# A transformer block on one core: later parts of the modulation loaded at longer intervals and summed later, splits of q, k, v first in line, both tiles' first norm ahead

## Chip, cores and metric

The kernel runs on one core of one Trainium2 chip. The metric is device time of one execution in microseconds (us), as the median of several runs. The profile is one execution, recorded by the hardware profiler; its times are microseconds from the start of its span.

## What is computed

One block over 256 tokens of width 1024, in float32. A vector `c` is turned into six rows of 1024 numbers, which shift, scale and gate the two halves of the block:

```python
mod = silu(c) @ w_ada + b_ada
sh_m, sc_m, gt_m, sh_f, sc_f, gt_f = split(mod, 6)
h = rms_norm(x, g_mix) * (1 + sc_m) + sh_m
qa, ka, va, qb, kb, vb, gate_logits = split(h @ w_in)    # six times 512, and 2048
oa = moba_attention(qa, ka, va, rel_bias)     # 8 heads, one block of 256: causal softmax with a bias
ob = stick_breaking_attention(qb, kb, vb)     # 8 heads
g_a, g_b = split(sigmoid(gate_logits))
mixed = (g_a * (oa @ w_br_moba) + g_b * (ob @ w_br_sb)) @ w_out
x = x + gt_m * mixed
h2 = rms_norm(x, g_ffn) * (1 + sc_f) + sh_f
u_val, u_gate = split(causal_conv3(h2 @ w_up))           # 2 times 2816
x = x + gt_f * ((gelu(u_gate) * u_val) @ w_down)
return rms_norm(x, g_final)
```

## The kernel before

**Precision.** Each float32 matrix is split into a high part (a cast to fp32r on ACT: `wh_`, `hh`, `qk` and so on) and a low part (the rest, subtracted on DVE: `wl_`, `hl`). A product is three matmuls on PE: high by high, high by low, low by high (`mm3`, L166). `split` (L144, L145) does it for weights, `hilo` (L150, L151; with a scale L153, L154) for what PE leaves in PSUM.

**Phase A**, up to about 63 us, is ordered by hand (`manual_schedule`, L63). `square` (L326) and `turn` scale each of the two token tiles by its norm and transpose it into `xT`. Then, for each of eight blocks of 128 columns, `row_sums` and `column_sums` make the first norm's shift and scale from `w_ada`, `modulated` (L444) makes `hh`, and `products` multiplies by rows of `w_in` (loaded as `raw_wA`) into the PSUM banks `pA` (q and k of the moba heads) and `pV` (v).

**From there on** a scheduler orders the instructions of each engine, by priorities that follow the order in which the code issues them. An engine takes its instructions strictly in that order. A `Stream` of units feeds PE: gate0, gate1, qkb0 and qkb2 (q and k of the stick-breaking heads, pairs 0 and 1, then 2 and 3), vb, gate2, gate3, ya, yb, out, up, down. A unit is two blocks of 128 rows of weights; `Stream.ahead` splits weights two units ahead. Weights come through three buffers `raw`. One unit on one token tile (or on one half, for qkb) is one event, and after each event `tick` lets every task under way take a step. Tasks are generators; `yield n` puts the next step n events later. PSUM has pools of 3 banks (`mm`, the stream's results), 1 (`pp`) and 4 (`sm`, all else).

**The tasks that the change touches.** `moba_pair` (L598 and on) has four instances, pair 0 to 3: scores in PSUM, then on DVE the bias and the maximum (`mx`, L607 to L609), on ACT the exponential (`sb`, L612) and the normalisation (L616), transposes on PE, and a split into `ph` and `pl`. `QK.place` (L549) takes `ps_qkb`, the result of qkb0 or qkb2, out of its bank and splits it into the tile `qk`. The first half (q) and the second (k) have a bank each, so with three banks the second half of qkb2 needs the bank that the first half of qkb0 held. `v_operand` (L560) does the same for v.

`modulation` (L731) makes the later rows: gt_m (named gtm; by `bcast_part`, which spreads the sums over the partitions with two matmuls `bc_gtm` on PE, L723), shf and scf for the second norm (each ends in eight short matmuls on PE, `ps_shf` and `ps_scf`, L739), and after the out stage gtf. Each row is summed from eight loads of 512 KB of `w_ada`, issued by SP through a pool of two buffers (`adap`), in `ada_part`:

```python
for k in range(KT):
    while stream.events < starts[k]:
        yield 1
    w.append(adap.tile([P, D], F32, tag="ada", name=f"ada_{nm}{k}"))
    pin(nc.sync.dma_start(w[k], w_ada[k * P:(k + 1) * P, base:base + D]))
    if k:
        mac(k - 1)
yield 3
mac(KT - 1)
```

`mac` is one DVE instruction over 128x1024 (`acc_gtm`, `acc_shf`, `acc_scf`; L696 for the first, L698 for the other seven). In the out stage `out_put` adds the residual, and makes the second norm, which uses `ps_shf` and `ps_scf` through the tile `ab2`.

## Time and profile before

| | us |
|---|---|
| median of 3 runs | 431.73 (431.01 to 436.56) |
| the profiled execution, device time | 431.41 |
| its span, first to last instruction | 429.7 |
| PE busy | 407.5 |
| DVE busy | 318.5 |
| ACT busy | 255.6 |

The device time of the profiled execution is 1.7 us over its span, and 0.3 us under the median. In a timeline row the numbers are start and duration; what stands in brackets is the idle time of that engine just before and what ended it. Durations of matmuls are modelled and overlap; the distance between two starts is what one costs. PEclk is TensorE's granted clock, 1.00 being 2.4 GHz and 0.50 being 1.2 GHz.

### The profile page before, as it was taken

Reading aid. Unit: us, or ns where it says so; the run is one execution under the profiler, and the core shown is the slowest. Engines: PE = TensorE matmul, PEld = TensorE weight load, DVE = VectorE, ACT = ScalarE, POOL = GpSimd, SP = SyncE. Lnnn points to the kernel's source line nnn. Section 1 sums busy time; section 2 is a strip of 40 time slices with the busy share of each in tenths; the row PEclk is TensorE's granted clock in tenths of the full one; section 3 lists DMA queues with packets and bytes.
Section 4 is the critical chain, followed back from the end, with each engine's and each line's share of the span. In section 5 each row is a group of like instructions: output and inputs, shape, how many; then the busy total and the mean of one; then the engine's idle time right before and its main releaser. Section 6 shows DMA issues by size and latency. Waiting matters only on the chain.

```text
span 429.7 us, 6803 instructions
## 1 busy us (share of the span) xinstructions
PE 407.5 (95%) x2636; PEld 357.5 (83%) x2636; DVE 318.5 (74%) x476; ACT 255.6 (59%) x407; POOL 25.1 (6%) x62
## 2 busy tenths in 40 slices
PE   7898999999699899999997999999999999999993
PEld 6786887899598787888875899999999999888882
DVE  2745578896779877997668779999898888546333
ACT  4425577875777779934355758666676666433312
POOL 2700000000001000000041000000000000000001
PEclk9999999999699999999998999999999999999997
DMA  8999988996368384775646685777376555573102
GB/s 275 333 319 333 356 306 290 327 309 223 125 237 300 112 286 146 274 238 224 194 123 221 188 299 201 233 255 261 135 217 202 174 194 195 151 276 116 45 2 98
DMA packets 67912, 94.45 MB, mean 220 GB/s; under 512 B 2573, under 2 KB 46736, under 8 KB 67879
## 3 DMA queue, kind: packets, MB, share of 16 engines
q1 hardware_dynamic: 66967, 91.82, 65.3%
q10 hardware_dynamic: 576, 1.57, 1.0%
q0 software_dynamic: 336, 0.62, 0.4%
q8 instruction: 21, 0.34, 0.3%
q14 instruction: 12, 0.10, 0.1%
HBM read 92.94 MB, written 1.06 MB: 219 GB/s over the span
## 4 chain that ended last, share of the span: by engine, by line
PE 60%; DMA 13%; DVE 12%; ACT 9%; issue 4%; POOL 1%; SPq 0%; POOLq 0%; DVEq 0%; ACTq 0%
PE ps_up L258 21%; PE ps_down L170 14%; DMA ada_gtm<-in_w_ada_dram 5%; PE pA L407 5%; PE ps_out L170 4%; DMA ada_shf<-in_w_ada_dram 4%; PE ps_up L170 3%; PE ps_ya L170 3%; PE ps_yb L170 3%; PE pV L412 2%; DMA raw_wA<-in_w_in_dram 2%; PE cs L392 2%; DMA ada_gtf<-in_w_ada_dram 2%; PE warm L121 2%; DVE wl_gate L145 1%
## 5 line engine op out<-in xcount | busy, mean ns | idle before, releaser
L144 ACT CAST wh_up<-raw_up 128x1024 fp32r<-128x1024 f32 x44 | 46.1, 1049 | 26.3 <-PE ps_up L258 20.5
L258 PE MATMUL ps_up<-h2h__2317,wh_up 128*128 128x256 f32 x320 | 57.7, 282 | 0.0
L258 PE MATMUL ps_up<-h2l__2318,wh_up 128*128 128x256 f32 x320 | 57.4, 281 | 0.0
L258 PE MATMUL ps_up<-h2h__2317,wl_up 128*128 128x256 f32 x320 | 57.4, 281 | 0.0
L145 DVE TENSOR_TENSOR wl_up<-raw_up,wh_up 128x1024 fp32r<-128x1024 f32 x42 | 51.0, 1218 | 7.7 <-ACT wh_up L144 7.5
L258 PEld LDWEIGHTS ps_up<-h2h__2317,wh_up 128*128 128x128 f32 x320 | 46.4, 188 | 0.2
L258 PEld LDWEIGHTS ps_up<-h2l__2318,wh_up 128*128 128x128 f32 x320 | 46.3, 188 | 0.0
L258 PEld LDWEIGHTS ps_up<-h2h__2317,wl_up 128*128 128x128 f32 x320 | 46.3, 188 | 0.0
L145 DVE TENSOR_TENSOR wl_down<-raw_down,wh_down 128x1024 fp32r<-128x1024 f32 x22 | 26.9, 1224 | 25.5 <-ACT wh_down L144 25.5
L144 ACT CAST wh_down<-raw_down 128x1024 fp32r<-128x1024 f32 x22 | 23.1, 1050 | 32.2 <-PE ps_down L170 23.7
L939 DVE SCALAR_TENSOR_TENSOR cv<-ps_up,wc,cv 128x255 f32<-128x255 f32 (+1 forms) x80 | 34.3, 475 | 1.3 <-ACT cv L933 0.8
L170 PE MATMUL ps_down<-wh_down,hl_a 128*128 128x512 f32 x88 | 34.8, 395 | 0.0
L170 PE MATMUL ps_down<-wl_down,hh_a 128*128 128x512 f32 x88 | 34.8, 395 | 0.0
L170 PE MATMUL ps_down<-wh_down,hh_a 128*128 128x512 f32 x88 | 34.8, 395 | 0.0
L170 PE MATMUL ps_gate<-wh_gate,hh 128*128 128x512 f32 x64 | 26.1, 407 | 1.2 <-DVE vbl L151 1.2
L170 PE MATMUL ps_gate<-wl_gate,hh 128*128 128x512 f32 x64 | 25.2, 394 | 0.0
L170 PE MATMUL ps_gate<-wh_gate,hl 128*128 128x512 f32 x64 | 25.2, 396 | 0.0
L933 ACT ACTIVATE cv<-ps_up,vc,wc 128x256 f32<-128x256 f32 x40 | 20.4, 564 | 5.2 <-PE ps_up L258 5.2
L145 DVE TENSOR_TENSOR wl_gate<-raw_gate,wh_gate 128x1024 fp32r<-128x1024 f32 x16 | 19.4, 1226 | 1.6 <-ACT wh_gate L144 1.6
L487 ACT CAST whA<-raw_wA 128x1024 fp32r<-128x1024 f32 (+1 forms) x9 | 8.5, 949 | 19.9 <-DMA raw_wA<-in_w_in_dram 19.9
L170 PEld LDWEIGHTS ps_down<-wh_down,hl_a 128*128 128x128 f32 x88 | 16.5, 188 | 4.0
L170 PEld LDWEIGHTS ps_down<-wh_down,hh_a 128*128 128x128 f32 x88 | 16.6, 188 | 3.9
(270 smaller groups left out, 899.4 us busy)
## 6 DMA issues: line engine op xcount, KB each, us to landing
raw_up<-in_w_up_dram SPq DMA_DIRECT2D x44, 512.0 KB, 5.1
raw_down<-in_w_down_dram SPq DMA_DIRECT2D x10, 1024.0 KB, 5.1
ada<-in_w_ada_dram SPq DMA_DIRECT2D x16, 512.0 KB, 7.4
raw_gate<-in_w_in_dram SPq DMA_DIRECT2D x8, 1024.0 KB, 5.1
raw_wA<-in_w_in_dram SPq DMA_DIRECT2D x8, 768.0 KB, 9.2
raw_qkb<-in_w_in_dram SPq DMA_DIRECT2D x8, 512.0 KB, 6.6
ada_gtm<-in_w_ada_dram SPq DMA_DIRECT2D x8, 512.0 KB, 4.7
ada_shf<-in_w_ada_dram SPq DMA_DIRECT2D x8, 512.0 KB, 6.5
```

The source lines that it names most:

```text
L121: nc.tensor.matmul(warm[:, 0:P], ones, ident, start=True, stop=True)
L144: nc.scalar.copy(wh[:, :n], t[:, a:a + n])
L145: (lo or nc.vector).tensor_sub(wl[:, :n], t[:, a:a + n], wh[:, :n].bitcast(F32))
L170: nc.tensor.matmul(ps, sx(k)[:, sl], w[:, c0:c0 + n], start=first and i == 0, stop=last and i == 2)
L258: nc.tensor.matmul(st.ps[f // 2][:, f % 2 * S:(f % 2 + 1) * S], wi[:, kk * 512 + f * P:kk * 512 + (f + 1) * P], sx(k0 + kk), start=first a ...
L392: nc.tensor.matmul(cs[g, 0:S].rearrange("p (i f) -> p i f", i=2), cw[:, k, :], ads[j][:, :, k, :], start=k < 4, stop=k >= 4)
L407: nc.tensor.matmul(psqk[f // 2][:, f % 2 * S:(f % 2 + 1) * S], wp[0][n == 2][:, f * P:(f + 1) * P], (hh, hl, hh)[n][:, j, :], start=j == 0 ...
L412: nc.tensor.matmul(psv[t], (hh, hl, hh)[n][:, j, t * P:(t + 1) * P], wp[1][n == 2][:, 0:512], start=j == 0 and n == 0, stop=j == KT - 1 an ...
L487: nc.scalar.copy(wh[i][:, a:a + n], wws[j][:, i * 1024 + a:i * 1024 + a + n])
L933: nc.scalar.activation(ct[:, b, :], tp[:, b * S:(b + 1) * S], AF.Identity, bias=bconv[:, fb:fb + 1], scale=wc[:, 88 + fb:89 + fb])
L939: nc.vector.scalar_tensor_tensor(ct[:, b, d:], tp[:, b * S:(b + 1) * S - d], wc[:, (2 - d) * 44 + fb:(2 - d) * 44 + fb + 1], ct[:, b, d:], ...
```

## The change

Four edits. `turn` no longer copies: both token tiles are scaled and transposed first, into the banks of `mm` (before: of `sm`), and the copies to `xT` come later (`put_xT`); a `warm_up(4)` between them is gone, and the banks `pA` and `pV` are taken after that. In `ada_part` the sum of load k-1 comes two events behind the issue of load k (before: at once), and the last one four events behind (before: three). The splits in `QK.place` and `v_operand` get a higher priority. The loads start at events 2 + int(3.2 i) (before: 3 + int(2.5 i)), i counting the 24 loads of gtm, shf and scf.

```diff
-    def turn(t, ss, copy):
+    def turn(t, ss):
         r = rstd_of(ss, f"n1_{t}")
         for half in range(2):
             sl = slice(half * 512, (half + 1) * 512)
             nc.vector.tensor_scalar(xs[t][:, sl], xs[t][:, sl], r, None, op0=ALU.mult)
+        tps = [bank(mm, f"xt{t}{half}") for half in range(2)]
+        for j in range(KT):
+            nc.tensor.transpose(tps[j // 4][:, j % 4 * P:(j % 4 + 1) * P], xs[t][:, j * P:(j + 1) * P], ident)
+        return tps
+
+    def put_xT(t, tps, copy):
         for half in range(2):
-            tp = bank(sm, f"xt{t}{half}")
-            for a in range(4):
-                j = 4 * half + a
-                nc.tensor.transpose(tp[:, a * P:(a + 1) * P], xs[t][:, j * P:(j + 1) * P], ident)
-            copy(xT[:, 4 * half:4 * half + 4, t * P:(t + 1) * P], tp.rearrange("p (a b) -> p a b", a=4))
+            copy(xT[:, 4 * half:4 * half + 4, t * P:(t + 1) * P], tps[half].rearrange("p (a b) -> p a b", a=4))
...
-    psqk = [bank(mm if i else pp, f"pA{i}") for i in range(4)]
-    psv = [bank(sm, f"pV{t}") for t in range(NT)]
+    psqk, psv = [], []
...
-    turn(0, ss1[0], nc.scalar.copy)
+    xt = [turn(t, ss1[t]) for t in range(NT)]
+    put_xT(0, xt[0], nc.scalar.copy)
...
     row = row_sums(0)
-    warm_up(4)
-    turn(1, ss1[1], nc.vector.tensor_copy)
+    put_xT(1, xt[1], nc.vector.tensor_copy)
...
     wp, hi, lo = w_parts(0)
+    psqk.extend(bank(mm if i else pp, f"pA{i}") for i in range(4))
+    psv.extend(bank(sm, f"pV{t}") for t in range(NT))
...
-            hilo(*(tile_[:, m:m + n, :].rearrange("p a (b c) -> p (a b) c", c=P) for m in (at, KT // 2 + at)),
+            with tc.high_priority(offset=150):
+                hilo(*(tile_[:, m:m + n, :].rearrange("p a (b c) -> p (a b) c", c=P) for m in (at, KT // 2 + at)),
                  tokens(ps, 2 * n, back), 0.125 if what == "q" else None)
...
         def put(t, ps):
-            hilo(vh[:, t, :], vl[:, t, :], ps)
+            with tc.high_priority(offset=150):
+                hilo(vh[:, t, :], vl[:, t, :], ps)
...
             if k:
+                yield 2
                 mac(k - 1)
-        yield 3
+        yield 4
         mac(KT - 1)
...
-    spawn(modulation([3 + int(2.5 * i) for i in range(3 * KT)]))
+    spawn(modulation([2 + int(3.2 * i) for i in range(3 * KT)]))
```

What this does to the order of the instructions is shown at three places. First DVE, around the maximum `mx` of moba pair 3 (`mx_1191` before, `mx_1181` in the changed kernel); the last two rows before, and the last one after, take `ps_qkb` of qkb0 out of its bank. Before:

```order
L607 ISA sb_1190,mx_1191<-s_1137,toep 128x128
L607 ISA mx_1191 128x1
L715 TENSOR_TENSOR acc_gtm<-acc_gtm,gt_m 1x1024
L609 TENSOR_SCALAR mx_1191<-mx_1191 128x4
L145 TENSOR_TENSOR wl_qkb_6_1347<-raw_qkb_4_1043,wh_qkb_6_1346 128x1024
L614 RECIPROCAL su_1192<-su_1192 128x4
L151 TENSOR_TENSOR oa_775<-po_m_1214,oa_774 64x256 x2
L630 TENSOR_TENSOR pl_1238<-pt_1239,ph_1237 128x384
L630 TENSOR_TENSOR pl_1238<-pt_1244,ph_1237 128x384
L145 TENSOR_TENSOR wl_vb_1419<-raw_vb_1154,wh_vb_1418 128x1024
L154 SCALAR_TENSOR_TENSOR qk_1273<-ps_qkb_0_1087,qk_1273 128x512
L151 TENSOR_TENSOR qk_1273<-ps_qkb_1_1120,qk_1273 128x512
```

Changed:

```order
L612 ISA mx_1181 128x1
L614 TENSOR_SCALAR mx_1181<-mx_1181 128x4
L703 SCALAR_TENSOR_TENSOR acc_gtm<-ada_gtm_1279,ca,acc_gtm 128x1024
L619 RECIPROCAL su_1182<-su_1182 128x4
L721 TENSOR_TENSOR acc_gtm<-acc_gtm,gt_m 1x1024
L151 TENSOR_TENSOR oa_771<-po_m_1206,oa_770 64x256
L145 TENSOR_TENSOR wl_qkb_6_1329<-raw_qkb_4_1038,wh_qkb_6_1328 128x1024
L151 TENSOR_TENSOR oa_771<-po_m_1206,oa_770 64x256
L145 TENSOR_TENSOR wl_vb_1398<-raw_vb_1146,wh_vb_1397 128x1024
L635 TENSOR_TENSOR pl_1230<-pt_1231,ph_1229 128x384
L635 TENSOR_TENSOR pl_1230<-pt_1236,ph_1229 128x384
L154 SCALAR_TENSOR_TENSOR qk_1264<-ps_qkb_0_1080,qk_1264 128x512
```

Before, all eight sums of gtm and the addition to row 0 (L715) stand ahead of `mx`; in the changed kernel the eighth sum and the addition (L721) stand behind it; the split `wl_vb`, which stood behind the two `pl`, now stands ahead of them, so that nothing but `pl` is left between it and `qk`.

Second ACT, from the normalisation of the same pair to the first split of `ps_qkb`. Before, the cast `wh_qkb_6` stands four exponentials ahead of the first row shown:

```order
L150 CAST oa_774<-po_m_1214 64x256
L616 ACTIVATE sb_1190<-sb_1190,su_1192 128x256
L616 ACTIVATE sb_1190<-sb_1190,su_1192 128x128
L150 CAST oa_774<-po_m_1214 64x256
L616 ACTIVATE sb_1190<-sb_1190,su_1192 128x256
L626 CAST ph_1237<-pt_1239 128x384
L626 CAST ph_1237<-pt_1244 128x384
L616 ACTIVATE sb_1190<-sb_1190,su_1192 128x128
L144 CAST wh_vb_1418<-raw_vb_1154 128x1024
L153 ACTIVATE qk_1273<-ps_qkb_0_1087 128x512
L652 ACT_TABLE_LOAD
L150 CAST qk_1273<-ps_qkb_1_1120 128x512
```

Changed, from behind the last exponential on:

```order
L144 CAST wh_qkb_6_1328<-raw_qkb_4_1038 128x1024
L621 ACTIVATE sb_1180<-sb_1180,su_1182 128x256
L150 CAST oa_770<-po_m_1206 64x256
L621 ACTIVATE sb_1180<-sb_1180,su_1182 128x128
L621 ACTIVATE sb_1180<-sb_1180,su_1182 128x256
L621 ACTIVATE sb_1180<-sb_1180,su_1182 128x128
L150 CAST oa_770<-po_m_1206 64x256
L144 CAST wh_vb_1397<-raw_vb_1146 128x1024
L631 CAST ph_1229<-pt_1231 128x384
L631 CAST ph_1229<-pt_1236 128x384
L657 ACT_TABLE_LOAD
L153 ACTIVATE qk_1264<-ps_qkb_0_1080 128x512
```

The cast `wh_qkb_6` and the load of a function table now stand between the exponentials and the split of `ps_qkb_0`; the copies of `bc_gtm` into `gt_m` have gone further back, and with them the matmuls `bc_gtm` on PE, from the first half of qkb2's first unit to behind the last matmuls of its two halves.

Third PE, at `ps_scf`, eight short matmuls with a row of ones. Before, between the units of yb:

```order
L170 MATMUL ps_yb_0_2068<-wl_yb_2_2044,ob_776 128x512
L170 MATMUL ps_yb_0_2068<-wh_yb_2_2043,ob_777 128x512
L739 MATMUL ps_scf<-ones,acc_scf 128x1 x8
L170 MATMUL ps_yb_0_2104<-wh_yb_0_2064,ob_776 128x512
L170 MATMUL ps_yb_0_2104<-wl_yb_0_2065,ob_776 128x512
```

Changed, behind the last unit of the out stage's first token tile and ahead of the second tile's:

```order
L170 MATMUL ps_out_0_2233<-wl_out_6_2247,zh 128x512
L170 MATMUL ps_out_0_2233<-wh_out_6_2246,zl 128x512
L745 MATMUL ps_scf<-ones,acc_scf 128x1 x8
L170 MATMUL ps_out_1_2322<-wh_out_0_2185,zh 128x512
L170 MATMUL ps_out_1_2322<-wl_out_0_2186,zh 128x512
```

`ps_shf` has moved in the same way, from gate3 into ya. On SP the loads of gtm, shf and scf stand further back among the loads of weights: the seventh of gtm, which stood ahead of the first `raw_vb`, now stands right behind it, and the last of scf stands behind the first `raw_up`.

## Rows read from the trace of the kernel before

**Rows 1.** The page's first part: busy time, share of the span, instructions, by engine.
```profile
PE 407.5 (95%) x2636; PEld 357.5 (83%) x2636; DVE 318.5 (74%) x476; ACT 255.6 (59%) x407; POOL 25.1 (6%) x62
```

**Rows 2.** Waits of PE: line, releaser: us in total, times, longest.
```profile
PE ps_qkb L258 <- DVE qk L154: 3.9, 1, 3.9
...
PE ps_up L170 <- ACT h2h__2317 L150: 2.3, 1, 2.3
...
PE pA L407 <- ACT hh L444: 1.7, 2, 1.4
...
PE ps_gate L170 <- DVE vbl L151: 1.2, 1, 1.2
...
PE cu L666 <- DVE lkl L661: 1.0, 1, 1.0
```

**Rows 3.** Costliest groups of the page: ACT's casts of the first weights.
```profile
L487 ACT CAST whA<-raw_wA 128x1024 fp32r<-128x1024 f32 (+1 forms) x9 | 8.5, 949 | 19.9 <-DMA raw_wA<-in_w_in_dram 19.9
```

**Rows 4.** Windows: busy us (instructions) of PE, PEld, DVE, ACT, POOL; PEclk, DMA share, GB/s.
```profile
3.00:57.00 54.00, 51.05 (x417) 42.84 (x418) 28.13 (x53) 24.13 (x51) 10.10 (x39) 1.00 1.11 337
...
112.00:118.00 6.00, 6.00 (x26) 5.71 (x27) 4.77 (x5) 3.75 (x6) 0.00 (x0) 0.51 0.27 73
...
200.00:210.00 10.00, 10.00 (x51) 8.23 (x50) 9.11 (x13) 4.85 (x6) 0.00 (x0) 1.00 0.39 115
...
226.00:228.00 2.00, 1.49 (x11) 1.30 (x11) 2.00 (x4) 1.09 (x3) 0.00 (x0) 1.00 0.98 343
...
231.00:233.00 2.00, 2.00 (x6) 1.47 (x6) 2.00 (x5) 0.68 (x3) 0.33 (x1) 0.50 1.11 383
```

**Rows 5.** Timeline of PE around the longest wait: start, duration, instruction, [idle before].
```profile
105.84 0.40 PE L258 MATMUL ps_qkb<-hh,wl_qkb 128*128 128x256 f32 x2
...
106.08 0.40 PE L258 MATMUL ps_qkb<-hl,wh_qkb 128*128 128x256 f32 x2
...
107.03 1.02 PE L723 MATMUL bc_gtm<-acc_gtm,ones 128*128 128x512 f32 x2
...
111.93 0.79 PE L258 MATMUL ps_qkb<-hh,wh_qkb 128*128 128x256 f32 x2 [3.87 <-DVE qk L154]
...
112.52 0.63 PE L258 MATMUL ps_qkb<-hh,wl_qkb 128*128 128x256 f32 x2
...
112.95 0.63 PE L258 MATMUL ps_qkb<-hl,wh_qkb 128*128 128x256 f32 x2
```

**Rows 6.** Timeline of ACT, 96 to 112 us.
```profile
96.87 1.98 ACT L144 CAST wh_qkb<-raw_qkb 128x1024 fp32r<-128x1024 f32 x2
...
104.01 0.51 ACT L612 ACTIVATE sb<-sb,mx 128x256 f32<-128x256 f32 x1 [5.16 <-DVE mx L609]
...
109.91 0.61 ACT L153 ACTIVATE qk<-ps_qkb 128x512 fp32r<-128x512 f32 x1
...
110.53 1.28 ACT L652 ACT_TABLE_LOAD   x1
```

**Rows 7.** Timeline of DVE, 99 to 112 us.
```profile
99.14 1.29 DVE L698 SCALAR_TENSOR_TENSOR acc_gtm<-ada_gtm,ca,acc_gtm 128x1024 f32<-128x1024 f32 x1 [2.14 <-DMA ada_gtm<-in_w_ada_dram]
...
102.69 1.21 DVE L715 TENSOR_TENSOR acc_gtm<-acc_gtm,gt_m 1x1024 f32<-1x1024 f32 x1
...
103.83 0.15 DVE L609 TENSOR_SCALAR mx<-mx 128x4 f32<-128x4 f32 x1
...
111.19 0.68 DVE L154 SCALAR_TENSOR_TENSOR qk<-ps_qkb,qk 128x512 fp32r<-128x512 f32 x1
```

**Rows 8.** Timeline of SP's DMA queue, 88 to 93 us.
```profile
88.94 0.75 SPq L317 DMA_DIRECT2D raw_vb<-in_w_in_dram  x1
...
92.62 0.33 SPq L704 DMA_DIRECT2D ada_gtm<-in_w_ada_dram  x1
```

**Rows 9.** Timeline of PE in the second half of yb.
```profile
192.19 1.84 PE L739 MATMUL ps_scf<-ones,acc_scf 128*128 128x1 f32 x16
```

**Rows 10.** Timeline of DVE in the out stage.
```profile
215.11 1.23 DVE L145 TENSOR_TENSOR wl_out<-raw_out,wh_out 128x1024 fp32r<-128x1024 f32 x1 [1.60 <-ACT wh_out L144]
```

## Prediction

> **What bounds the kernel.** I read the busy times first. PE is busy 407.5 of 429.7 us [rows 1], so the end is set by PE, and a change can win only PE's idle time (429.7 less 407.5, 22.2 us), its half-speed time, or work that PE is spared. Next the waits of PE [rows 2]: apart from the first microseconds, the longest is 3.9 us, on the split of q (`qk`, L154) by DVE; then 2.3 on the second norm (`h2h`), twice up to 1.4 in phase A on `hh`, 1.2 on `vbl` before gate2, and 1.0 on `lkl`. Last the windows, which show what a wait costs beyond itself [rows 4]: behind the 3.9 us wait the granted clock is 0.51 in the mean from 112 to 118, in effect all of it at 1.2 GHz, and behind the second norm it is 0.50 again from 231 to 233.
>
> The long wait read as a chain, backwards. PE starts again at 111.93 [rows 5] when DVE's split at 111.19 has ended. ACT's half of it started at 109.91 [rows 6], and DVE's came 0.7 after ACT's had ended, behind a split of weights (`wl_vb` in the order shown); ACT had been busy without a gap since 104.01, after 5.16 idle in which it waited for `mx`. `mx` started at 103.83 on DVE [rows 7], behind the addition to row 0 of gtm's sum (102.69, 1.21 long), behind the eighth sum of gtm (99.14), which itself waited 2.14 for its load. So PE waits, four steps on, for loads and sums of `w_ada` that nobody needs yet.
>
> **Start (edit of the first norm): 0.** PE starts its products earlier, by at most the work that goes from between the two tiles, as an estimate 1.5 us, the size of the longer wait on `hh` (1.4 [rows 2]). But the loads decide from there: ACT's casts `whA` wait 19.9 us in seven places for `raw_wA` [rows 3], and the DMA engines are busy with a share of 1.11 from 3 to 57 us [rows 4]. An earlier start makes PE wait longer at the next load. I take 0; bounds -1.5 and, since no work is added, 0.
>
> **The long wait.** Two things happen. DVE gets to `mx` earlier, and ACT's list from `mx` to `qk` gets longer.
> - DVE: one sum (1.29 long, the last 0.1 beside the next instruction) and the addition (102.69 to 103.83, 1.14) are no longer in front of `mx` [rows 7]: 103.98 (its end) becomes 101.64. The sum that is now just in front belongs to the seventh load. That one stands behind `raw_vb`, issued at 88.94 with a duration of 0.75, while the load that DVE waited for was issued at 92.62 [rows 8]: up to 2.9 us earlier, so the wait of 2.14 can go wholly: 99.5. Against that stands ACT, whose two casts `wh_qkb` from 96.87 (0.99 each) [rows 6] give DVE its next split no earlier than 97.9, and from there a split (1.22), the four maxima (1.1, what is left of 99.14 to 102.69 behind one sum and one split) and `mx` (0.15) make 100.3. I take 100.0; ends 97.5, if all loads come early, and 103.98, if nothing is gained.
> - ACT from `mx`: in before the split started 5.90 behind the first exponential (109.91 less 104.01) [rows 6], some 0.3 of it waiting for the reciprocal. Now `wh_qkb_6` (0.99) comes into it, filling that wait, and the table load (1.28): 5.90 - 0.30 + 0.99 + 1.28 = 7.87. To this 0.03 for the start, 0.5 until DVE may follow (an estimate from the split's 0.61), 0.68 for DVE's half and 0.06 to PE: 9.1 behind `mx`. (Before, it was 111.93 - 103.98 = 7.95, with the 0.7 behind `wl_vb` in it, which is now ahead of `pl` and out of the way.) So PE resumes at 100.0 + 9.1 = 109.1 in place of 111.93: -2.8.
> - The two pairs of `bc_gtm` (0.46 each, the end of the second at 108.05) leave the place in front of this wait, where they were hidden, for one where PE is dense: +0.9. PE therefore comes to the wait at some 106.8, and idles 2.3.
>
> Net -1.9; in general, end of `mx` less 101.9. It pays only if `mx` ends before 101.9; with `mx` at 103.98 it costs 2.1.
>
> **The clock behind it: -2.6.** The distance of two starts is 0.24 before (105.84 to 106.08) and 0.43 after the wait (112.52 to 112.95) [rows 5]. From 111.93 to nearly 118 that is 5.9 us for the work of 5.9 x 0.24 / 0.43 = 3.3, a loss of 2.6. Idle times of 1.4, 1.2 and 1.0 [rows 2] left the clock at full; 3.87 cost it; 2.3 on `h2h` cost it too, but PE had already been busy only 1.49 of the 2 us from 226 to 228 [rows 4], while it is dense before this one. 2.3 us lies between. I take that the clock stays, and keep 0 as the other end.
>
> The Trainium skill speaks against me here: "Perfetto Trace Analysis", Matmul Optimizations, says that the matmul engine scales its power with its utilization, so matmuls should come back to back in batches. By that rule alone a gap of 2.3 us would still cost the clock, and the sum would be 2.6 higher; this trace agrees with it at 3.87 and disagrees at 1.4, and has no row of a lone gap between them.
>
> **Smaller terms.** The wait on `vbl` (1.2 [rows 2]) goes: in the changed order five sums of shf stand in front of it and not eight, 1.2 us each, and its split has priority; -1.1, bounds -1.2 and 0. `ps_scf` (1.8, in dense yb [rows 9]) goes to the out stage, where PE afterwards waits 2.3 for the second norm [rows 2]: it eats into that wait, -1.8. `ps_shf`, the same eight matmuls, does the reverse: it stood ahead of the wait on `lkl` (1.0 [rows 2]) and now stands behind it, in ya. If `lkl` comes no earlier, PE waits for it 1.8 longer and pays the matmuls afterwards: +1.8. Together 0; bounds -1.8, if `lkl` comes earlier by as much, and +1.8, if the second norm's chain is late by what PE is. The second clock drop [rows 4] stays, since no edit shortens the norm's chain: 0; bound -1.3, some 3 us at half speed times the lost share of 1 - 0.24 / 0.43. The sums of scf move into yb and out, where DVE is busy 9.11 of 10 from 200 to 210 [rows 4]: some six sums, 7 us. That stretch has room for less than one, its neighbours must take the others, and the 1.60 that DVE is idle ahead of a `wl_out` [rows 10] is such room: 0; bounds 0 and +2, a sum and a half that finds none.
>
> **Sum.** 0 - 1.9 - 2.6 - 1.1 + 0 = -5.6 against the profiled execution's 431.4, hence 425.8; that execution was 0.3 under the median, so 426.0 as the median, rounded.
>
> **Rivals.**
> - *The clock falls all the same.* For it: the gap of 2.3 on `h2h` with 0.50 behind it. Against it: a dense PE before. Then only -1.9 and -1.1 are left: 428.7.
> - *The wait goes altogether.* If `mx` ends by 97.5, PE never stops: it goes on at 106.6 (107.03 less the first pair of `bc_gtm`) in place of 111.93, -5.3, pays 0.9 for `bc_gtm` later, and keeps the 2.6 and the 1.1: -8.1, or 423.6; if the second clock drop goes as well (-1.3) and the start is worth 1.5, 420.8. For it: DVE's 2.14 on a load shows that it was loads which set its pace, and each sum now stands two events further behind its load. Against it: ACT's casts, which put `mx` at 100.3.
> - *The sums hold up the out stage.* The eighth sum of scf now stands in front of DVE's last split `wl_out`, which in before began at 215.11 after 1.60 idle [rows 10]. Its load stands behind the first `raw_up`. If it lands later than about 215, PE waits for each microsecond; 2 us give 428.
> - *Slower.* The seventh load, now behind `raw_vb`'s megabyte, lands no earlier than the eighth did, `mx` stays at 103.98, and the longer ACT list decides: PE resumes at 113.1, the gap grows to 6 us, and the clock falls as before. That is +2.1 - 1.1 = +1.0, 432.7; with `ps_scf` not hidden either 434.5. For it: the eighth load took until 99.1 from its issue at 92.62 [rows 7, 8], 6.5 us. It decides from `mx` at 103.0 on.
>
> **Chances and range.** Forecast 0.45; clock falls 0.2; wait gone 0.15; sums hold up 0.08; slower 0.12. The lower end takes in the wait gone with the second drop and the start, and some more of the second norm's wait: 420.5. The upper end takes in the clock lost with a part of the slower case: 432.0. Two per cent is 8.6 us, about what a measurement of this kernel can tell from no change; faster than that is below 423.1, which only the wait gone, with something besides, and the lower edge of the forecast reach: 0.18. Slower by as much needs 440.4, which no case reaches: 0.03. Within: 0.79.
>
> **What would show it.** Right: the wait of `ps_qkb` on `qk` falls to between 1 and 3 us, `mx` of pair 3 ends near 100, PEclk stays 1.00 from 106 to 118, `ps_gate` no longer waits on `vbl`, `ps_scf` stands where PE waits afterwards. Wrong: 0.50 behind the shorter wait; `mx` later than 102; a new wait of `ps_out` on `wl_out`, or of `ps_scf` on `acc_scf`; or a first product that starts earlier and a phase A that really ends earlier.

## The result, and the profile of the changed kernel

The changed kernel is slower by about one per cent: 436.81 us (median of 20 runs, 432.90 to 440.27) beside 432.69 us of the kernel before (20 runs, 428.49 to 436.56); ratio 1.0096, interval 1.0066 to 1.0125. The forecast was 426.0, the range ended at 432.0, and the sign is wrong: some 4 us lost in place of 5.6 won. The profiled execution took 433.11 us with a span of 431.4, the second fastest of its 20; that has to be kept in mind with everything it shows. Ratios, and means over runs, leave out the runs that are more than 1.5% above the fastest of their kernel (two of the 20).

The page's busy times:

```profile
PE 404.5 (94%) x2628; PEld 353.0 (82%) x2628; DVE 316.4 (73%) x476; ACT 255.7 (59%) x407; POOL 25.5 (6%) x62
```

PE is busy for 3.0 us less than in [rows 1], since it ran at half speed less in this execution, and still the span is 1.7 longer: PE's idle time went from 22.2 to 431.4 less 404.5, 26.9. The waits say where (line, releaser: us in total, times, longest):

```profile
PE pA L408 <- ACT hh L445: 4.1, 3, 2.6
PE ps_qkb L258 <- DVE qk L154: 2.8, 1, 2.8
PE ps_gate L170 <- ACT gate L765: 2.5, 1, 2.5
...
PE cu L671 <- DVE lkl L666: 2.3, 1, 2.3
PE ps_up L170 <- ACT h2h__2313 L150: 2.3, 1, 2.3
PE ps_gate L170 <- DVE vbl L151: 1.4, 1, 1.4
```

Beside [rows 2]: the long wait of `ps_qkb` is 1.0 shorter. The one of `cu` on `lkl` has more than doubled, and there is one of 2.5 us that did not exist before: `ps_gate` on ACT's copy `gate`. `vbl` and `h2h` are as before. The windows at the two places where the clock had fallen before [rows 4] (busy us of PE, PEld, DVE, ACT, POOL; PEclk, DMA share, GB/s):

```profile
112.00:118.00 6.00, 6.00 (x54) 5.63 (x53) 4.40 (x7) 3.60 (x8) 0.14 (x1) 1.00 0.56 187
...
234.00:237.00 3.00, 2.73 (x11) 1.80 (x10) 2.53 (x7) 0.49 (x1) 0.94 (x1) 1.00 0.93 325
```

The granted clock is 1.00 at both, all 2.4 GHz. Worked out from the first instruction of each stage on PE, with a second execution of the changed kernel from the experiments (`e4_after`, 440.54 us, the slowest of its six) beside it, the spans divide so:

```
stage (first start to first start)   before   after   e4_after
start to ps_gate (phase A)            62.87    65.33    66.40
ps_gate to ps_vb (gate1, qkb)         66.50    62.81    66.24
ps_vb to cu                            9.51     9.51     9.52
cu to ps_ya (vb, gate2, gate3)        38.33    40.89    42.80
ps_ya to ps_yb                        12.25    14.02    14.02
ps_yb to ps_out                       13.68    11.83    11.83
ps_out to h2t (out)                   23.37    24.93    24.94
h2t to ps_up (second norm)             4.09     4.09     4.09
ps_up to ps_down                     129.92   128.87   129.89
ps_down to the end                    69.18    69.12    69.07
```

Three things are to be read from it. `ps_gate` to `ps_vb`, the stretch with the long wait, won 3.7 us in the profiled execution and 0.3 in the other. From `cu` to `ps_ya` both lost, 2.6 and 4.5. And `ps_scf` did move 1.8 us out of yb, but 1.57 of it came back in the out stage. Phase A is taken up with the first experiment.

### The profile page after: what moved, and what is told of

Its sections match the earlier page's. It is cut to its first block, busy times and chain, and to the rows that moved or that the text cites. A ratio compares the mean times of both kernels' runs of the same rounds, so it can differ in the third digit from the quotient of the medians.

```text
span 431.4 us, 6784 instructions
## 1 busy us (share of the span) xinstructions
PE 404.5 (94%) x2628; PEld 353.0 (82%) x2628; DVE 316.4 (73%) x476; ACT 255.7 (59%) x407; POOL 25.5 (6%) x62
## 3 DMA queue, kind: packets, MB, share of 16 engines
q10 hardware_dynamic: 576, 1.57, 1.0%
## 4 chain that ended last, share of the span: by engine, by line
PE 61%; DMA 11%; ACT 10%; DVE 8%; issue 5%; POOL 2%; SPq 0%; POOLq 0%; DVEq 0%; ACTq 0%
PE ps_up L258 26%; PE ps_down L170 14%; DMA raw_wA<-in_w_in_dram 4%; PE pA L408 4%; DMA ada_gtm<-in_w_ada_dram 3%; PE ps_ya L170 3%; PE ps_qkb L258 2%; PE ps_up L170 2%; PE pV L413 2%; DMA ada_shf<-in_w_ada_dram 2%; PE ps_yb L170 2%; PE cs L393 2%; DMA raw_up<-in_w_up_dram 1%; PE ps_gate L170 1%; ACT wh_gate L144 1%
## 5 line engine op out<-in xcount | busy, mean ns | idle before, releaser
L144 ACT CAST wh_up<-raw_up 128x1024 fp32r<-128x1024 f32 x44 | 46.2, 1050 | 27.5 <-PE ps_up L258 19.7
L258 PEld LDWEIGHTS ps_up<-h2l__2314,wh_up 128*128 128x128 f32 x320 | 46.2, 188 | 0.0
L145 DVE TENSOR_TENSOR wl_down<-raw_down,wh_down 128x1024 fp32r<-128x1024 f32 x22 | 26.9, 1223 | 25.5 <-ACT wh_down L144 25.5
L491 DVE TENSOR_TENSOR wlA<-raw_wA,whA 128x1024 fp32r<-128x1024 f32 x8 | 9.8, 1224 | 13.7 <-ACT whA L488 13.7
```

The lines of the kernel that those rows point to most:

```text
L144: nc.scalar.copy(wh[:, :n], t[:, a:a + n])
L145: (lo or nc.vector).tensor_sub(wl[:, :n], t[:, a:a + n], wh[:, :n].bitcast(F32))
L258: nc.tensor.matmul(st.ps[f // 2][:, f % 2 * S:(f % 2 + 1) * S], wi[:, kk * 512 + f * P:kk * 512 + (f + 1) * P], sx(k0 + kk), start=first a ...
L491: nc.vector.tensor_sub(wl[i][:, a:a + n], wws[j][:, i * 1024 + a:i * 1024 + a + n], wh[i][:, a:a + n].bitcast(F32))
```

## The experiments

Twelve kernels ran, in four groups, each beside the kernel before on the same chip. What was expected is quoted as it stood before each ran.

**e1_norm**: the kernel before with the edit of the first norm alone.

```diff
+    xt = [turn(t, ss1[t]) for t in range(NT)]
+    put_xT(0, xt[0], nc.scalar.copy)
...
-    warm_up(4)
-    turn(1, ss1[1], nc.vector.tensor_copy)
+    put_xT(1, xt[1], nc.vector.tensor_copy)
```

> Only the edit of the first norm: both tiles scaled and transposed first, the warm_up(4) between them gone. Theory M (the loss comes from the later sums, through a gate stage in which ACT sets the pace and from matmuls of ps_scf that hide nothing): the same time as before, within 0.3%, the first pA about 1.5 us earlier, the first ps_gate where it was (63 us). Theory N (the loss is the first norm's): 1% slower (+4 us), PEclk under 0.8 from 15 to 17 us, the first ps_gate 2.4 us later than before, as in the changed kernel's profile (65.3 against 62.9).

432.60 us beside 431.36; ratio 1.0026, interval 0.9993 to 1.0059. The first product `pA` starts at 13.66 us in place of 15.69, and `ps_gate`, the first after phase A, at 63.25 in place of 62.87: 2.0 us won at the start are waited for again in phase A. Over the profiles `ps_gate` starts with the new first norm (five of them) between 63.25 and 66.40, at 64.9 in the mean, with the old one (nine) between 62.87 and 67.00, at 64.6 in the mean. The 2.5 us of the pair in the table above are therefore not put down to the change.

**e2_mod**: the kernel before with the new starts and the two later sums alone.

```diff
             if k:
+                yield 2
                 mac(k - 1)
-        yield 3
+        yield 4
...
-    spawn(modulation([3 + int(2.5 * i) for i in range(3 * KT)]))
+    spawn(modulation([2 + int(3.2 * i) for i in range(3 * KT)]))
```

> Only the edits of ada_part and of the starts. Theory M: about the changed kernel's time, +2 to +4 us over before, with its two waits in the gate stages (ps_gate on the copy of a gate 2.5 us, cu on lkl 2.3) and the long wait of ps_qkb at 2.8 in place of 3.9. Theory N: 1 to 3 us faster than before, since the long wait shrinks and nothing is lost elsewhere that ps_shf's 1.8 do not pay.

435.27 us; ratio 1.0088, interval 1.0050 to 1.0126. A loss of the changed kernel's size (1.0096 above, 1.0138 in e4) is here with neither of the other edits. Its waits of PE:

```profile
PE ps_qkb L258 <- DVE qk L154: 5.0, 1, 5.0
PE ps_gate L170 <- ACT gate L760: 2.5, 1, 2.5
...
PE cu L666 <- DVE lkl L661: 2.3, 1, 2.3
```

The two waits of the gate stages are those of the changed kernel's first profile to the tenth (in e4 they are 3.1 and 0.7), and its `ps_scf` costs the out stage the same 1.57. Here even the long wait grew. DVE's timeline shows how (start, duration, instruction, [idle before]):

```profile
105.17 1.28 DVE L698 SCALAR_TENSOR_TENSOR acc_gtm<-ada_gtm,ca,acc_gtm 128x1024 f32<-128x1024 f32 x1 [2.71 <-DMA ada_gtm<-in_w_ada_dram]
106.37 0.17 DVE L614 RECIPROCAL su<-su 128x4 f32<-128x4 f32 x1
```

The eighth sum had been taken from in front of `mx`, and stood then between `mx` and the reciprocal `su`, on the same chain to the split of q: DVE works in order, and waited 2.71 us for the sum's load there.

**e3_prio**: the kernel before with the priority of the splits alone.

```diff
+            with tc.high_priority(offset=150):
+                hilo(*(tile_[:, m:m + n, :].rearrange("p a (b c) -> p (a b) c", c=P) for m in (at, KT // 2 + at)),
...
+            with tc.high_priority(offset=150):
+                hilo(vh[:, t, :], vl[:, t, :], ps)
```

> Only the priority of the splits of q, k and v. Its order of instructions differs from before in few places, and bc_gtm, ps_shf and ps_scf stay where they were. Both theories: the time of before within 0.3%. Faster by over 1 us would say that the split of q ahead of the table load alone shortens the wait of 3.9 us.

433.36 us; ratio 1.0029, interval 0.9996 to 1.0062. Its waits:

```profile
PE ps_gate L170 <- DVE vbl L151: 2.0, 1, 2.0
PE ps_qkb L258 <- DVE qk L154: 1.8, 1, 1.8
PE ps_vb L170 <- DVE qk L154: 1.3, 1, 1.3
```

The long wait fell from 3.9 to 1.8, more than in any kernel with late sums, and the clock behind it stayed. What took its place was a wait of 1.3 at the next split and 2.0 on `vbl`, behind which a stretch at half speed followed; over 12 runs nothing is left.

**e4_after**: the changed kernel once more, beside these three.

> The changed kernel once more, for a second profile on the same chip as the single edits. Theory M and N: +3 to +5 us over before. If its granted clock is lower than the 0.991 of the first profile, the time over before at equal clock is the idle time of PE, 4.7 us more than before; a drop of the clock behind the waits of 2.3 to 2.8 us in gate3, at cu or at ps_qkb adds about 2.6 each.

437.24 us; ratio 1.0138, interval 1.0091 to 1.0184. Waits:

```profile
PE ps_qkb L258 <- DVE qk L154: 3.8, 1, 3.8
PE ps_gate L170 <- ACT gate L765: 3.1, 1, 3.1
```

and the window behind the first of them:

```profile
115.00:121.00 6.00, 6.00 (x37) 5.54 (x37) 3.40 (x5) 2.38 (x6) 0.00 (x0) 0.72 0.57 190
```

Here the clock did fall: 0.72 behind the `ps_qkb` wait of 3.8, and again behind the gate wait of 3.1 and behind the second norm. The first profile, read alone, would have passed for a proof that the clock was won.

**e5_gtm_only**: the changed kernel, with the starts and the sums of shf and scf as before, so that gtm alone is late. It was to tell whether the place of gtm, or that of shf and scf, costs the time.

```diff
             if k:
-                yield 2
+                if nm == "gtm":
+                    yield 2
                 mac(k - 1)
-        yield 4
+        yield 4 if nm == "gtm" else 3
...
-    spawn(modulation([2 + int(3.2 * i) for i in range(3 * KT)]))
+    spawn(modulation([2 + int(3.2 * i) if i < KT else 3 + int(2.5 * i) for i in range(3 * KT)]))
```

> The changed kernel with the loads and sums of shf and scf at the times of before; gtm stays late, the first norm and the priority stay changed. ps_shf is in gate3 again and ps_scf in yb, as before. Theory P (the loss is where ps_shf and ps_scf went): out to the second norm's first transposes back from 24.9 to 23.4 us, the wait of ps_gate on the copy of a gate from 2.5 to under 1, 3 us less than the changed kernel, so within 0.4% of before. Theory L (the late gtm with its waits of 2 to 3 us is itself the loss, by the clock): no better than the changed kernel by more than 1 us, +0.7% or more over before.

439.30 us beside 431.85; ratio 1.0163, interval 1.0120 to 1.0206. For `ps_scf` the expectation held: it is back in yb, and the out stage takes 23.37 us as before. For the total it failed. The wait on the copy `gate` is gone, but the others are not (waits of PE):

```profile
PE ps_qkb L258 <- DVE qk L154: 3.6, 1, 3.6
...
PE cu L671 <- DVE lkl L666: 3.2, 1, 3.2
```

and GpSimd's mask of the stick-breaking pairs, `zs`, is slow twice:

```profile
154.70 1.75 POOL L644 TENSOR_SCALAR_AFFINE_SELECT zs<-zs 128x256 f32<-128x256 f32 x2 [19.93 <-ACT zs L652]
166.64 2.69 POOL L644 TENSOR_SCALAR_AFFINE_SELECT zs<-zs 128x256 f32<-128x256 f32 x2 [10.19 <-ACT zs L652]
```

gtm was not late alone. `modulation` begins shf only when gtm is through, whatever the event of shf's loads says, and so the sums of shf run here from 131.3 to 154.8 us, as in the changed kernel (127.8 to 156.6) and not as before (115.0 to 140.6). The experiment does not tell the place of gtm from that of shf. It turned the question from the events to what DVE does beside the mask.

**e6_gtm_alone**: the same on the kernel before, without the other two edits.

```diff
-    spawn(modulation([3 + int(2.5 * i) for i in range(3 * KT)]))
+    spawn(modulation([2 + int(3.2 * i) if i < KT else 3 + int(2.5 * i) for i in range(3 * KT)]))
```

> Before, with only gtm loaded at longer intervals and summed later; nothing else is changed. Theory P: the long wait at ps_qkb shrinks by 1 us or more and bc_gtm costs 0.9, so -2 to 0 us against before. Theory L: +0.5% or more, as in the run with all of the modulation's edits (+0.9%).

436.59 us; ratio 1.0094, interval 1.0058 to 1.0129. The edits of gtm alone give a loss of the changed kernel's size; priority and norm are not needed for it. The sums of shf are late here too, by the same order of `modulation`: 132.8 to 156.6.

**e7_busy_dve**: the kernel before with four more DVE instructions of 128x256 beside the mask of the third pair (`hp == 2`); one operand is in SBUF, the other, `z`, in PSUM.

```diff
+        if hp == 2:
+            with tc.high_priority(offset=150):
+                for _ in range(4):
+                    nc.vector.scalar_tensor_tensor(scr, scr, ca[:, 0:1], z[1][:, 0:256], op0=ALU.mult, op1=ALU.add)
```

> Before, with four extra DVE instructions of 128x256 on a scratch tile (they read scores in PSUM) placed around the split wl_gate beside GpSimd's mask of zs for stick-breaking pair 2, so that DVE has no gap there. Theory B (GpSimd's mask gets on only in gaps of DVE): the mask takes 2.5 us or more in place of 1.05, and ACT's Abs behind it starts 1.5 to 2 us later; the chain of pair 2 is late by as much at the next copy of a gate. Rival (the mask was long in the changed kernel for another reason, its input's time): the mask keeps 0.8 to 1.1 us, and nothing behind it moves but by DVE's own 1.5 us.

One run, 435.69 us. The mask, and the one of the four that stands beside it:

```profile
151.66 1.05 POOL L641 TENSOR_SCALAR_AFFINE_SELECT zs<-zs 128x256 f32<-128x256 f32 x2 [13.87 <-ACT zs L649]
...
152.01 0.48 DVE L654 SCALAR_TENSOR_TENSOR scr<-scr,ca,z 128x256 f32<-128x256 f32 x1
```

The mask takes 1.05 (1.07 in the kernel before). That DVE is merely busy is not enough; this account falls. With one instruction of 0.48 beside the mask the case is thin by itself; the other traces, below, bear it out.

**e8_no_shf_sums**: the changed kernel without the second to the eighth sum of shf.

```diff
         def mac(k):
+            if k and nm == "shf":
+                return
```

> The changed kernel without the second to eighth sum of shf on DVE (the loads and ps_shf stay; shf is wrong by those seven parts). Theory S (these sums, now in the gate stages, hold up the stick-breaking chain on DVE and GpSimd's mask, and ACT's copy of a gate behind it): the mask of pair 2 back from 2.8 to 1.1 us, the wait of ps_gate on the copy of a gate under 1 us, and from the first cu to the first ps_ya 38.5 us or less in place of 40.9; 2 to 4 us under the changed kernel. Rival (PE waits there because ps_shf's 1.8 are gone from it and ACT's pace is what it was): the wait stays at 2 us or more and the stretch at 40 or more.

431.17 us beside 432.14; ratio 1.0004, interval 0.9964 to 1.0043: the loss of the changed kernel is gone. The waits on `gate` and on `vbl` are gone, the one on `lkl` stays (2.1), and from `cu` to `ps_ya` it takes 36.28 us, 4.6 less than the changed kernel. GpSimd's masks:

```profile
147.54 1.05 POOL L644 TENSOR_SCALAR_AFFINE_SELECT zs<-zs 128x256 f32<-128x256 f32 x2 [14.60 <-ACT zs L652]
157.79 0.77 POOL L644 TENSOR_SCALAR_AFFINE_SELECT zs<-zs 128x256 f32<-128x256 f32 x2 [9.20 <-ACT zs L652]
```

The stretch is under 40 and the wait is gone, so the rival is out, and without these sums the loss is gone. The kernel before has them too, and was not run without them, but its trace shows what they cost there: seven of the eight stand ahead of the first `cu` (115.0 to 135.3, the eighth at 140.65), and from `cu` to `ps_ya` it takes 38.33 us with the 1.84 of `ps_shf` in it, so some 36.5 without, beside 36.28 here. In that stretch they cost before next to nothing, so that it is their new place which costs.

**e9_busy_dve2**: as e7, with both operands in SBUF.

```diff
+                nc.vector.tensor_copy(scr[:, 0:1], z[1][:, 0:1])
+                for _ in range(4):
+                    nc.vector.scalar_tensor_tensor(scr, scr, ca[:, 0:1], scr, op0=ALU.mult, op1=ALU.add)
```

> Before, with extra DVE instructions around the split wl_gate beside GpSimd's mask of zs for pair 2, as in the run before, but four of 128x256 whose two operands both lie in SBUF (ahead of them one of 128x1 that reads PSUM). Theory C (the mask gets on only while DVE has no instruction with two operands in SBUF): the mask takes 2 us or more in place of 1.05, and ACT's Abs behind it starts later by as much. Rival (the mask's length has to do with something else): 1.05 again.

One run, 431.53 us. Mask and DVE:

```profile
148.30 1.28 POOL L641 TENSOR_SCALAR_AFFINE_SELECT zs<-zs 128x256 f32<-128x256 f32 x2 [13.94 <-ACT zs L649]
...
148.64 0.15 DVE L653 COPY scr<-z 128x1 f32<-128x1 f32 x1
148.83 0.49 DVE L655 SCALAR_TENSOR_TENSOR scr<-scr,ca 128x256 f32<-128x256 f32 x1
149.23 1.43 DVE L147 TENSOR_TENSOR wl_gate<-raw_gate,wh_gate 128x1024 fp32r<-128x1024 f32 x1
```

The mask grew to 1.28 and not beyond 2 as expected, and `wl_gate` beside it took 1.43 in place of 1.22. The row of the mask is two instructions, and its second began at 148.95, while the first of the four (148.83 to 149.31) was under way; it ended at 149.58, 0.27 behind that one, and took 0.64 in place of 0.40. The theory holds for it. The size is smaller than expected because only one of the four came to stand beside the mask; that is a fault of the experiment. What it leaves open is a mask held up on purpose by the 1.8 us that it lost in the changed kernel.

**e10_pairs_early**, **e11_pairs_mid_prio**, **e12_pairs_mid**: another way to shorten the long wait, with the loads as in the kernel before: moba pairs at events 2 + 4 hp or 2 + int(4.5 hp) in place of 2 + 5 hp; in e11 with a priority of 400 for the splits too.

```diff
-    spawn(heads(moba_pair, qka, va, oah, oal, [2 + 5 * hp for hp in range(NHP)]))
+    spawn(heads(moba_pair, qka, va, oah, oal, [2 + int(4.5 * hp) for hp in range(NHP)]))
```

> Before, with the moba pairs started at events 2, 6, 10 and 14 in place of 2, 7, 12 and 17; the modulation stays as it was. The maximum of pair 3 comes some 6 us earlier, ACT's list from it to the split of q keeps its length. If the long wait of ps_qkb is set by when that maximum ends: the wait falls from 3.7 (mean of four profiles) to under 1 us, PE does not lose the work in front of it as with the late gtm, and the time is 2 to 5 us under before. If the wait is set by the sequence on ACT, whatever starts it: 3 us or more stay, and the time of before within 0.4%.

> Before, with the moba pairs started at events 2, 6, 11 and 15, and the splits of q, k and v at a high priority (offset 400). A try at a better version, from what the runs show: leave the sums where they are, and bring the maximum of pair 3 forward instead. If the long wait goes without the waits on s and po_m that starts at 2, 6, 10, 14 brought (1.4 and 2.0 us): 1 to 3 us under before. If the waits only change their place again: within 0.4% of before.

> The same without the priority. If the priority matters for vbl and qk, 0.5 to 1.5 us slower than with it; else the same time.

e10: 431.52 beside 432.14, ratio 0.9990, interval 0.9959 to 1.0022. The wait of `ps_qkb` is gone, and others have come, 2.9 on `vbl`, 1.4 on `mx` and 2.0 of `po_m`; the 2 to 5 us that were expected did not.

e12: 431.60 beside 432.46, ratio 0.9966, interval 0.9935 to 0.9997. e11: 429.91, ratio 0.9940, interval 0.9906 to 0.9974, faster than both kernels, by 0.6% beside the kernel before. In its profile the 3.9 us before the second half of qkb have become

```profile
PE ps_vb L170 <- DVE qk L154: 3.1, 1, 3.1
```

one split later. PE's idle time is 22.2 there as before; that execution was the slowest of its 12, so it does not show what was won. The mean granted clock over runs does: 0.9904 in e11, 0.9865 in the kernel before beside it. From [rows 5], a microsecond at half speed loses 1 - 0.24 / 0.43 = 0.44, and the time at half speed is twice what the mean lacks to 1: 3.6 us lost against 5.1, so 1.5 of the 2.6 us between their means. Only the difference counts: in every profile the clock is at half speed again in the last microseconds of the span, where PE has done its last matmul (before: from 425.0, and PE ends at 422.2), and that part of either figure is no loss. Where the other 1.1 come from was not settled.

## Why the prediction was wrong, point by point

**Start: right.** In e1 two microseconds earlier (at most 1.5 had been forecast), and nothing at the end of phase A. One thing stays open: in two of the five profiles with the new first norm (after, from 14.2 to 17.8 us, and e8) the clock was at half speed near the first products, and in none of the nine with the old one.

**The long wait: the chain was right, the gain was not.** The three parts of the timeline of the changed kernel, DVE and ACT and PE:

```profile
101.92 0.17 DVE L614 TENSOR_SCALAR mx<-mx 128x4 f32<-128x4 f32 x1
...
102.12 0.51 ACT L617 ACTIVATE sb<-sb,mx 128x256 f32<-128x256 f32 x1 [2.71 <-DVE mx L614]
...
110.26 0.60 ACT L153 ACTIVATE qk<-ps_qkb 128x512 fp32r<-128x512 f32 x1
...
111.63 0.51 PE L258 MATMUL ps_qkb<-hh,wh_qkb 128*128 128x256 f32 x2 [2.83 <-DVE qk L154]
```

ACT idles 2.71 before the exponentials in place of 5.16 [rows 6], and its list from there to the split of q is longer, as worked out. In microseconds from the first `ps_gate`, so that phase A drops out:

```
kernel      PE arrives   mx ends   mx to resume   PE resumes   idle
before        45.19       41.11        7.95          49.06      3.87
e1_norm       45.21       39.88        9.54          49.42      4.21
e7            45.59       40.61        7.96          48.57      2.98
e9            45.55       40.86        7.96          48.82      3.27
e3_prio       45.21       38.36        8.62          46.98      1.77
after         43.47       36.76        9.54          46.30      2.83
e4_after      44.35       38.62        9.54          48.16      3.81
e2_mod        43.49       37.59       10.92          48.51      5.02
e5            43.48       37.54        9.55          47.09      3.61
e6            43.48       37.14        9.54          46.68      3.20
e8            43.74       38.13        9.54          47.67      3.93
```

The upper five have early gtm sums, the lower six late ones. In the mean `mx` comes 2.5 earlier (forecast 4.0) and the list is 1.4 longer (forecast 1.2), so PE resumes 1.2 earlier (forecast 2.8). PE also arrives 1.7 earlier (forecast 1.3). The wait itself is 3.2 in the mean of the five and 3.7 in that of the six. The profiled execution of the changed kernel, -2.8 at the resumption, is the best of the six. Late sums are also not all that moves the two: e1, whose gtm is early, has the longer list of 9.54 as well (`wh_qkb` and the table load stand in ACT's row there too), and e3 has an early `mx`.

The step that failed is "PE therefore comes to the wait at some 106.8, and idles 2.3". Counted from `ps_gate` as in the table, PE came when forecast (43.9; 43.7 in the mean of the six). It resumed at 47.4 in place of 46.2, because `mx` ended 0.5 later than the 100.0 that was taken and the list took 9.8 and not 9.1. Each of the two sides was known only to about a microsecond, and their difference was taken as if it were sharp.

**The clock: the term of -2.6 rested on that idle time and fell with it.** Of the waits of `ps_qkb`, those of 2.83 (after) and 1.8 (e3) left the clock at 1.00; behind each of the others, 2.98 and up, there is a stretch at half speed. So "the clock stays" at 2.3 is not refuted, but a wait of 2.3 is what this change does not give. The first rival (clock falls all the same) was the better case for this stretch, but because the wait is longer than 2.3, not because a wait of 2.3 costs the clock.

**The gate stages: the loss that no case had.** This is the largest term. It is read from the changed kernel's timeline, DVE, GpSimd, ACT and PE:

```profile
147.10 2.35 DVE L145 TENSOR_TENSOR wl_gate<-raw_gate,wh_gate 128x1024 fp32r<-128x1024 f32 x2
149.37 1.42 DVE L703 SCALAR_TENSOR_TENSOR acc_shf<-ada_shf,ca,acc_shf 128x1024 f32<-128x1024 f32 x1
150.71 0.54 DVE L675 TENSOR_TENSOR zs<-zs,cu 128x384 f32<-128x384 f32 x1
...
148.22 2.84 POOL L644 TENSOR_SCALAR_AFFINE_SELECT zs<-zs 128x256 f32<-128x256 f32 x2 [16.96 <-ACT zs L652]
...
151.09 0.85 ACT L658 ACTIVATE t<-zs 128x768 f32<-128x768 f32 x1 [2.96 <-POOL zs L644]
...
162.22 0.58 ACT L765 COPY gate<-ps_gate 128x512 f32<-128x512 f32 x1
...
162.86 0.50 PE L170 MATMUL ps_gate<-wh_gate,hh 128*128 128x512 f32 x1 [2.50 <-ACT gate L765]
...
172.05 0.44 PE L671 MATMUL cu<-lkl,tri 128*128 128x384 f32 x1 [2.29 <-DVE lkl L666]
```

In the kernel before the same stretch reads

```profile
148.02 1.07 POOL L639 TENSOR_SCALAR_AFFINE_SELECT zs<-zs 128x256 f32<-128x256 f32 x2 [13.88 <-ACT zs L647]
...
148.91 1.26 DVE L145 TENSOR_TENSOR wl_gate<-raw_gate,wh_gate 128x1024 fp32r<-128x1024 f32 x1 [0.45 <-ACT wh_gate L144]
...
149.12 0.85 ACT L653 ACTIVATE t<-zs 128x768 f32<-128x768 f32 x1 [0.25 <-POOL zs L639]
...
160.78 0.59 ACT L759 COPY gate<-ps_gate 128x512 f32<-128x512 f32 x1
```

There DVE had a gap of 0.45 between two splits, and GpSimd's mask, two instructions, was done in 1.07. In the changed kernel a late sum of shf fills DVE without a gap to 150.79, and the mask ends 0.27 behind it: 2.84, with 0.77 in e8 for the next pair's mask, which has no sum or split beside it. Counted from the first `cu` (at 138.88 before, 137.65 after), it also begins 1.4 later, 1.1 of that because in ACT's row a second cast `wh_gate` now stands ahead of the copy that the mask waits for (before and e8: behind it). So ACT, which waits 2.96 for the mask, takes up the pair's next step 3.2 later. ACT works in order, and the copy that frees the bank of `ps_gate` comes 2.7 later. Also `ps_shf`, 1.84 us of work that had covered this time on PE, has gone to ya. The sum from `cu` to `ps_ya`: -1.84 for `ps_shf`, +2.50 for the new wait, +1.3 on `lkl` and +0.2 on `vbl` are +2.2; measured +2.56. In e4 the same stretch lost 4.5, with 3.1 on the copy `gate`, 1.9 on `vbl`, 0.7 on `lkl`, and a stretch at half speed behind the 3.1.

The Trainium skill has a rule for this place, "SBUF — State Buffer", Who interferes with whom: a DVE instruction with two inputs in SBUF contends with a GpSimd instruction that reads SBUF; the first to start has the shared ports for the whole instruction, the other is blocked. This trace agrees: the mask ends 0.27 behind DVE's run of such instructions (`wl_gate`, `acc_shf`), at 2.84 for 0.77, `acc_shf` took 1.42 beside it where 1.28 is usual, and instructions with a PSUM operand left it at 1.05 (e7). So do the other traces. In the 14 there are 112 instructions of this mask. The 57 that began while DVE was idle, or in an instruction that reads PSUM, took 0.40 or 0.41. The 55 that began while DVE was in an instruction reading only SBUF ended 0.26 or 0.27 behind it (in after, e2 and e4 once behind the next one, which began together with the mask); only three, which began in its last 0.1 us, took 0.41 all the same. The first sum of scf, which has one input in SBUF, held the mask up too (0.68 for 0.41 in before).

That the sums of shf at their new place cost the time in the gate stages is shown by e8 with the trace of before; that such sums hold up the mask is shown by the traces together. How much of PE's loss goes through the mask's 1.8, and how much through DVE's own lateness and ACT's changed order, is read from the timelines, and was not shown by a kernel that changes the mask alone. The step that failed is in the smaller terms: of the sums of shf the prediction counted only those that no longer stand ahead of `vbl` (-1.1), and had no term for those that now run in the gate stages. DVE's sums were priced by DVE's own free time, for scf in yb and out, and what else had lived in DVE's gaps was never asked.

**vbl: wrong.** It was to go (-1.1); it is 1.4 and 1.9 in the two profiles of the changed kernel. In e8 it is gone. Three fewer sums in front were not enough, because the two nearest ones, the fourth and the fifth, now stand directly ahead of the chain to `vbl`: DVE idles 1.15 us for the load of the fourth and sums from 138.38 to 140.98, so that `vbl` starts 6.2 us behind the first `cu`, beside 5.9 before, where one sum, the eighth, stood there, and 3.8 in e8.

**ps_scf: the step "it eats into that wait, -1.8" failed.** The out stage of the changed kernel, DVE, PE and ACT:

```profile
223.88 0.17 DVE L749 TENSOR_TENSOR ab<-ps_scf,b 128x8 f32<-128x8 f32 x1 [0.99 <-PE ps_scf L745]
223.96 1.03 DVE L854 TENSOR_TENSOR xr<-xr,xn 128x512 f32<-128x512 f32 x1
...
222.00 1.84 PE L745 MATMUL ps_scf<-ones,acc_scf 128*128 128x1 f32 x16
...
224.94 0.40 PE L170 MATMUL ps_out<-wh_out,zl 128*128 128x512 f32 x1
...
225.42 1.05 ACT L144 CAST wh_up<-raw_up 128x1024 fp32r<-128x1024 f32 x1 [2.45 <-issue]
226.37 0.63 ACT L855 ACTIVATE xn<-xr 128x512 f32<-128x512 f32 x1
```

The same places in the kernel before:

```profile
221.68 2.12 DVE L848 TENSOR_TENSOR xr<-xr,xn 128x512 f32<-128x512 f32 x1
...
221.91 0.40 PE L170 MATMUL ps_out<-wh_out,zl 128*128 128x512 f32 x1
...
222.40 1.05 ACT L144 CAST wh_up<-raw_up 128x1024 fp32r<-128x1024 f32 x1 [0.66 <-ACT xn L849]
...
223.84 0.63 ACT L849 ACTIVATE xn<-xr 128x512 f32<-128x512 f32 x1 [0.39 <-DVE xr L848]
```

The second norm hangs on the residual `xr` and then on its square, `xn` on ACT. The reader of `ps_scf`, `ab`, does stand ahead of `xr` in DVE's row, and DVE waits 0.99 there, but this costs nothing: counted from the first `ps_out` (203.14 before, 204.39 after), `xr` ends at 20.66 before and at 20.60 after. Before, it took 2.12 beside a split `wl_up` on GpSimd, and in both kernels it ends 0.55 behind that split. What is late is the square, at 20.70 before and 21.98 after. It stands on ACT behind a cast `wh_up`, which waits for the end of a matmul `ps_out` of the second token tile (222.31 before, 225.34 after; ACT's sequencer waits on that matmul's semaphore, and the cast begins 0.1 behind it). `ps_scf` stands ahead of that tile on PE, and so the matmul comes 1.8 later. The norm's chain is late by 1.57, and the wait behind it is 2.26 as before.

From `ps_out` to `h2t` it takes 23.34 to 23.37 in the ten kernels with `ps_scf` in yb, and 24.93 or 24.94 in the four with it in the out stage (after, e2, e4, e8): +1.57 against the -1.85 in yb. Of the other half of the pair, the 1.8 for `ps_shf` in ya came (+1.77), and so this part ends at +1.5 in place of 0. It was within the bounds (+1.8, "if the second norm's chain is late by what PE is"), with the wrong end taken.

**The sums of scf in yb and out: right.** No new wait on `wl_out`; this rival is out. So is the slower one by its mechanism: `mx` never stayed at its old place. That it forecast the sign was luck.

**The second clock drop: half.** The second norm's wait is 2.3 in every profile, and behind it the clock fell in before, e1, e3, e4, e6, e7, e10, e11 and e12, and stayed in after, e2, e5, e8 and e9. Over runs the mean granted clock is 0.982 in the changed kernel (18 runs, and again in the 6 of e4) and 0.9865 in the kernel before (26 runs beside e4). By the arithmetic given for e11 that is 7.1 us lost in place of 5.1, so +2.0. The means of e4 and of the kernel before beside it are 437.2 and 431.8; that leaves 3.3 us for waits. So more than a third of the loss is clock by this estimate: not one long drop more, but some four waits of 2 to 3 us, each of which now and then costs a stretch such as the one of e4 (six microseconds at 0.72, which is 6 x 2 x 0.28 = 3.4 at half speed, 1.5 lost). The mean clock of e8 is as low, 0.9815 over its 10 runs, at the time of the kernel before. So the low clock does not come from the sums of shf, and e8 wins as much elsewhere; where was not settled.

## What to carry to other kernels

Before work is moved into an engine's idle time, look at what other engines do just then: the gap in DVE's row was the time in which GpSimd's mask got through, and closing it cost PE more than the moved work was worth. A moved matmul makes the matmuls behind it late, and with them whatever waits for their end: here a cast on ACT, and the square that stood behind it in ACT's order. So follow what the later matmuls release, and see which wait ends last before blaming one: the reader of `ps_scf` waited in front of the same chain and cost nothing. And a forecast that hangs on the difference of two times, each known to a microsecond, should carry that uncertainty into everything behind it; one profile that comes out as hoped is not yet evidence, since the second one here did not.

## What the runs showed of the hardware that was not expected

GpSimd's mask of 128x256, twice, took anything from 0.77 to 2.84 us, by what DVE did beside it, and DVE's own instruction grew from 1.28 to 1.42, or from 1.22 to 1.43. It goes the other way round too: beside GpSimd's `wl_up` DVE's residual `xr` took 2.12 us, where the one ahead of it took 0.69.

Waits of the same length cost the clock in one execution and not in the next: the 2.3 us before `ps_up` (fell in nine profiles, stayed in five); 2.3 on `cu` in after (stayed) and e2 (fell); 1.9 on `vbl` in e4 (stayed) and e5 (fell). For a wait of 2 to 3 us a single profile of this kernel says nothing sure of the clock; the mean over runs does.
